# A hybrid decoder layer on one core: when retention starts, how decay tiles are made, and how the first loads are queued

## The chip, the core and the metric

The program runs on one core of a Trainium2 chip. The time is that of one execution in device microseconds (us), median of several; a profiled execution gives the trace. The engines are named as in the profile: PE (matrix products; PEld its weight loads), DVE (vector), ACT (scalar engine, with function tables that must be loaded), POOL and SP (SP issues most DMAs here, in order).

## The reference

One layer, 512 tokens of width 1024, all float32. After an RMS norm one wide projection feeds two token mixers: retention (8 heads) and a gated DeltaNet (8 heads, called DN below). Both are chunked, four chunks of 128 tokens. Their outputs are gated, merged and projected, and a gated MLP with a short causal convolution follows.

```python
u = rmsnorm(h, g_mix); proj = u @ w_in
rq, rk, rv, rgate, dq, dk, dv, dz, db, da, gate_r, gate_d = split(proj)
ro = retention_chunkwise(rotary(rq), rotary(rk) * RET_DK**-0.5, rv)     # 4 chunks, 8 heads
q, k, v = silu(causal_dwconv(concat(dq, dk, dv)))                       # then l2norm of q and k
G = cumsum(g); L[i, j] = exp(G_i - G_j) for i >= j                      # the decay tiles
A = strict_lower((beta * k) @ k.T * L)
u, w = triangular_solve(I + A, [beta * v, beta * k * exp(G)])           # the solve
# a scan over the four chunks then gives the DeltaNet output do
h += (sigmoid(gate_r) * (silu(rgate)*norm(ro) @ w_ret) + sigmoid(gate_d) * (norm(do)*silu(dz) @ w_dn)) @ w_o
h += (silu(a) * b) @ w_down ; a, b = split(causal_dwconv(rmsnorm(h) @ w_up) + bias); out = rmsnorm(h)
```

## The kernel before

Every product is made of three products of split halves: a float32 operand is cut into `hi` (a rounded copy, ACT) and `lo` (what is left, DVE), and PE adds hi·hi, hi·lo and lo·hi in a PSUM bank. Weights come in blocks of 128x1024 (`wraw`), issued by SP in the order of a fixed list and split to `whi` on ACT and `wlo` on DVE. Branch, output and down projections use a Strassen-like scheme with seven products, whose weight sums POOL's DMAs prepare.

The order of the instructions on PE, ACT, DVE and POOL is written down when the program is built. The class `Order` keeps a model clock; small tasks (Python generators) are queued with `spawn`, and after each dense product `poll` lets the tasks record their instructions whose model time has come. A number in a `yield` is a pause in model us, and a `while ...: yield 0.3` waits for a condition. On the chip each engine follows its recorded order and waits only for semaphores. So a changed pause or condition changes which instructions stand next to which, here from the start up to the end of the DN heads. SP's queue has eight semaphores in turn: a DMA is issued when the eighth DMA before it has landed and its own conditions hold.

The places that matter, in time:

- **Head.** `load_x` loads the rows of x transposed (tiles `xt0` to `xt7`, 256 KB each), `load_w` halves of the first two weight blocks, the rest comes in `load_rest`. `g_split` makes `ghi` and `glo` of one tile; in steps named in the dictionary `then` it also writes one column of a tile that is loaded next, by `act.copy`, and since the DMA into this tile must wait for that write, the later loads are held back until ACT is there. `square` feeds the row sums: tiles `sq` are added on DVE, and the matmul `pss` takes the sum. `ba_w` is a small weight that the products `pba` need.
- **DN heads**, two groups of four (GH = 4). Each head takes three weight blocks, products `pk`, `pq`, `pv`, a convolution and Silu (tiles `k`, `q`, `v`), and transposes on PE (`pkt`, `pqt`, `pvt`). `decay_tiles` spawns `decay_tile` for each head: a DMA broadcasts a row into `gb`, ACT makes |G_i - G_j| by four Abs (each with another bias) and then one Exp. Exp and Silu lie in different function tables, so a table is loaded (ACT_TABLE_LOAD) where they follow each other. DVE then builds the tile `A` from `pkk` and `gb`.
- **Solve.** For a group, `solve` runs 31 steps on DVE (the chain: `xtmp`, `xx`), sends the result through DRAM into `tt`, and `solve_up` joins the blocks with products `pm` in four rounds; `m` is their negated copy on DVE. Then two `scan` tasks, for two heads each (`psc`, `vn`, `Sn`), whose ends (`scan_end`) normalise `vtok`, transpose it (`pot`) and copy it with a scale to `doT` on ACT.
- **Retention.** The blocks of rq, rk and rv are products `pr` between the two groups. `ret_back` then does four pairs of heads, `ret_scores` (`prs`, `pkv`), `ret_state` (`rS`), `ret_out` (`pro`) and `ret_norm` (`ro`, `proT`, `roT`).

All PSUM tiles share eight banks; a new tile is given one that is free in the recorded order, and waits on the chip for the last reader of what was in it.

Of the kernel before, what the change touches and what calls it, by code (L numbers as in the profile page):

```python
# [11 lines left out]
F32 = mybir.dt.float32  # L12
F32R = mybir.dt.float32r
AF = mybir.ActivationFunctionType
# [5 lines left out]
P = 128  # L20
T = 512
D = 1024
NT = T // P
# [74 lines left out]
class Order:  # L98
# [29 lines left out]
    def spawn(self, gen, after=0.0):  # L128
        self.n += 1
        heapq.heappush(self.tasks, ((self.clock if self.now is None else self.now) + after, self.n, gen))  # L130
# [107 lines left out]
def body(nc, tc, ctx, io):  # L238
    sp = nc.sync
    order = Order()  # L240
    spawn, poll, hold = order.spawn, order.poll, order.hold
    vec = Engine(order, "vec", nc.vector, vec_cost)
    act = Engine(order, "act", nc.scalar, act_cost)
# [3 lines left out]
    const = ctx.enter_context(tc.tile_pool(name="const", bufs=1))  # L247
# [11 lines left out]
    def S(name, dt=F32):  # L259
        return heap.tile([P, T], dt, name=name, tag="s", bufs=HEAP)  # L260
# [10 lines left out]
    def v3(ap, n=4):  # L271
        return ap.rearrange("p (n f) -> p n f", n=n)
# [5 lines left out]
    def ck(n, f=P):  # L278
        return slice(n * f, (n + 1) * f)
# [8 lines left out]
    def fetch():  # L288

        while count["fetch"] < len(BLOCKS) and free[0]:  # L290
            free[0] -= 1
            i = count["fetch"]
            count["fetch"] += 1
            b = BLOCKS[i]
            n = 512 * b[4] if b[0] == "q" else D
            raw = wp.tile([P, n], F32, name="wraw", tag="wraw", bufs=RAWB)
            if b[0] == "q":
                sp.dma_start(raw, quarter(b[1], b[2])[:, 1024 * b[3]:1024 * b[3] + n])
            else:
                sp.dma_start(raw, io["w"][count["plain"]])  # L300
                count["plain"] += 1
            raws[i] = raw
# [203 lines left out]
    cst = const.tile([P, 256], F32, name="cst")  # L506
# [4 lines left out]
    ones = const.tile([P, P], F32, name="ones")  # L511
# [41 lines left out]
    xt = [S(f"xt{k}") for k in range(KT)]  # L553
# [5 lines left out]
    def load_x(*ks):  # L559
        for k in ks:  # L560
            sp.dma_start(xt[k], io["xt"][k])

    def load_w(i, n):
        sp.dma_start(first_raw[i][:, ck(n, T)], io["w"][i, :, ck(n, T)])

    def load_rest():
        sp.dma_start(cst[:, :P], io["cst"][:, :P])
        sp.dma_start(prm[:, P_CW:], io["prm"][:, P_CW:])
        fetch()
        sp.dma_start(cst[:, P:], io["cst"][:, P:256])  # L570
        sp.dma_start(alog, io["dn_a_log"].partition_broadcast(P))
        sp.dma_start(dtb, io["dn_dt_bias"].partition_broadcast(P))
        sp.dma_start(cst2, io["cst"][:, 256:])

    sp.dma_start(prm[:, :P_BA], io["prm"][:, :P_BA])
    load_x(0)
    load_w(0, 0)
    load_w(1, 0)
    load_x(1)
    sp.dma_start(prm[:, P_BA:P_CW], io["prm"][:, P_BA:P_CW])  # L580


    then = {0: (2, lambda: (load_x(2, 3), load_w(0, 1))), 1: (4, lambda: (load_x(4), load_w(1, 1), load_x(5))),
            2: (6, lambda: (load_x(6, 7), load_rest()))}


    warm = PS("warm")
# [9 lines left out]
    scale, row_scale_, minus = [], [], []  # L597

    def g_split(k):
        act.activation(ghi[k], xt[k], AF.Identity, scale=prm[:, P_GM + k:P_GM + k + 1])  # L600
        if k in then:
            tile_, load = then[k]
            act.copy(xt[tile_][:, :1], ones[:, :1])
            load()
        yield
        vec.scalar_tensor_tensor(glo[k], xt[k], prm[:, P_GM + k:P_GM + k + 1], ghi[k].bitcast(F32), ALU.mult, ALU.subtract)
        yield
        g_ready.add(k)
        spawn(square(k), 0.6)

    def square(k):
        sq = S("sq")
        act.activation(sq, xt[k], AF.Square, scale=1.0 / 32.0)
        yield
        squares.append(sq)
        if len(squares) > 1:
            vec.tensor_tensor(squares[0], squares[0], sq, ALU.add)
            yield
        if len(squares) == KT:
            yield from row_scales(squares[0])  # L620
# [72 lines left out]
    def hn(name):  # L693
        return const.tile([P, H, NT], F32, name=name)
# [4 lines left out]
    beta, G, nG, eG, egl, ekd = (hn(n) for n in ("beta", "G", "nG", "eG", "egl", "ekd"))  # L699
    g_dram = dram.tile([32, P], F32, name="g_dram")  # L700
# [75 lines left out]
    em, egb = {}, {}  # L776

    def row_of(d, h):
        return d[4 * h:4 * h + 4, :].rearrange("n f -> (n f)").partition_broadcast(P)

    def decay_tiles(hs):
        while "G" not in have:
            yield 0.3
        for h in hs:
            while h >= GH and "o" not in heads[h - GH]["got"]:
                yield 0.3
            spawn(decay_tile(h))
            yield 9.0 if h < GH else 4.0

    def decay_tile(h):  # L790
        gb = S(f"gb{h}")
        sp.dma_start(gb, row_of(g_dram, h))
        yield 6.0 if h < GH else 2.6
        for n in range(NT):
            act.activation(gb[:, ck(n)], gb[:, ck(n)], AF.Abs, bias=nG[:, h, n:n + 1])
        act.activation(gb, gb, AF.Exp, scale=-1.0)
        yield
        em[h] = gb

    def conv_silu(ps, ci, name):  # L800
        w = prm[:, P_CW + 4 * ci:P_CW + 4 * ci + 4]
# [11 lines left out]
    GH = 4  # L813
# [18 lines left out]
    heads = [dict(h=h, got=set()) for h in range(H)]  # L832


    keys = [0]
# [84 lines left out]
    def v_front(hd, ps):  # L920
# [8 lines left out]
            act.activation(hd["vtok"][:, ck(n)], pvt[:, ck(n)], AF.Identity, scale=hd["c1"][:, n:n + 1])  # L929
        hd["got"].add("v")  # L930

    def solve(g):

        group = heads[g * GH:(g + 1) * GH]
        while not all("k" in hd["got"] for hd in group):
            yield 0.3
        while g > 0 and not all("o" in hd["got"] for hd in heads[(g - 1) * GH:g * GH]):
            yield 0.3
        sa = [heap.tile([P, 32, 16], F32, name=f"sa{i}", tag="s", bufs=HEAP) for i in range(2)]
        adv = a_dram[g].rearrange("b h n i j -> (b h n) i j")  # L940
        for i in range(2):
            sp.dma_start(sa[i][:NP], adv[:, :, ck(i, 16)])
        xx = small.tile([P, 32, 32], F32, name="xx", tag="xx", bufs=1)
        tmp = small.tile([P, 256], F32, name="xtmp", tag="xtmp", bufs=1)
        pool.memset(xx[:NP], 0.0)
        pool.memset(xx.rearrange("p a b -> p (a b)")[:NP, ::33], 1.0)
        yield 8.0
        for j in range(31):
            shp = [NP, j + 1, 31 - j]
            a = sa[j // 16][:NP, j + 1:, j % 16].unsqueeze(1).to_broadcast(shp)  # L950
            tv, xv_ = v3(tmp[:NP, :(j + 1) * (31 - j)], j + 1), xx[:NP, :j + 1, j + 1:]
            vec.tensor_tensor(tv, a, xx[:NP, :j + 1, j:j + 1].to_broadcast(shp), ALU.mult)
            vec.tensor_tensor(xv_, xv_, tv, ALU.subtract)
            yield
        sp.dma_start(x_dram[g].rearrange("b h n i j -> (b h n) (i j)"), xx[:NP].rearrange("p a b -> p (a b)"))
        for b in range(4):
            sp.dma_start(tt_all[R32[b], :, R32[b]], x_dram[g][b].rearrange("h n j i -> j (h n) i"))
        yield 13.5
        spawn(solve_up(group))
# [191 lines left out]
    normed = []  # L1151
# [3 lines left out]
    def ret_scores(hp):  # L1155

        pss = [PS("prs") for _ in range(2)]
        for n in range(NT):
            for r, ps in zip(E64, pss):
                pe.matmul(ps[:, ck(n)], rkT[n][r, hp], rqT[n][r, hp], start=True, stop=True)  # L1160
        pk = PS("pkv")
        for n in range(NT - 1):
            for e, r in enumerate(E64):
                vv = rv[n][hp // 2][:, ck(2 * hp % 4 + e)]
                pe.matmul(pk[r, ck(n)], krot[n][:, hp, r], vv, start=True, stop=True)
        yield
        states[hp] = [None]
        sTs = [S("sT") for _ in range(2)]
        for sT, ps in zip(sTs, pss):
            vec.tensor_tensor(v3(sT), v3(ps), umask.unsqueeze(1).to_broadcast([P, NT, P]), ALU.mult)  # L1170
        return sTs, pk
# [58 lines left out]
    def ret_back():  # L1230
        while any(a is None for a in (*rqT, *rkT, *(b for a in rv for b in a))):
            yield 0.3
        for hp in range(4):

            while "up" not in heads[GH - 1]["got"] or len(normed) < 2 * hp or keys[0]:
                yield 0.3
            yield 1.5
            sTs, pk = yield from ret_scores(hp)
            yield from ret_state(hp, pk)
            spawn(ret_out(hp, sTs))  # L1240
            yield 8.0
# [23 lines left out]
    def scaled(front, hd, ps):  # L1265
# [5 lines left out]
        yield from front(hd, x)  # L1271

    spawn(decay_tiles(range(GH)))

    def dn_front(g):
# [7 lines left out]
    for front in (rq_front, rk_front, rv_front(0), rv_front(1)):  # L1283
        if front is rk_front:
            spawn(decay_tiles(range(GH, H)), 75.0)
        dense_r([PS("pr") for _ in range(NT)], g_tile, done=front)
    spawn(ret_back())
    dn_front(1)

# [498 lines left out]
```

## Time and profile before

| | us |
|---|---|
| median of 3 runs | 986.39 (984.97 to 987.19) |
| profiled execution | 986.46 |
| its span, first to last instruction | 984.7 |
| PE busy | 965.5 (98% of the span) |
| DVE, ACT, POOL busy | 747.3, 533.9, 166.7 |
| PE in the chain that ended last | 82% of the span |

The span is 1.8 us shorter than the profiled execution's own time. A row of the timeline has the start, the length, the engine, the line, the operation with output and inputs, and in brackets the idle time before it and what ended that. L200 and L235 are lines of helpers through which all instructions go, so groups are told apart by their tiles. The length of a pipelined matmul overlaps with the next one: what one costs in a row is read from start to start.

### The profile page before, as it was taken

The numbers are of one execution on the slowest core, as the hardware profiler recorded it, in microseconds if no ns is written. First come the engines' busy times: TensorE is split into PE (matmuls) and PEld (weight loads), VectorE is DVE, ScalarE is ACT, GpSimd is POOL, SyncE is SP. The second block draws the span as 40 slices with busy tenths as digits, with TensorE's granted clock in tenths as the row PEclk, the third lists the DMA queues.
The fourth block names the chain that finished last, engine by engine and source line by source line (L and its number), as shares of the span: only waits on it lengthen the run. The fifth ranks groups of instructions, "written<-read, shape, count | busy, mean of one in ns | idle before, by whom it ended". The sixth has DMA issues, their size and how long they took to land.

```text
span 984.7 us, 14107 instructions
## 1 busy us (share of the span) xinstructions
PE 965.5 (98%) x5133; PEld 804.9 (82%) x5133; DVE 747.3 (76%) x1359; ACT 533.9 (54%) x1113; POOL 166.7 (17%) x209
## 2 busy tenths in 40 slices
PE   8999999999899999999999999899999999999997
PEld 6887888888788888888888887788888888888886
DVE  6887799458788898675799889865656676678785
ACT  6589422265955433486786546754444333356663
POOL 0121312224443230132000000221122221000001
PEclk9999999999999999999999999999999999999999
DMA  8244569978788695479986754665579999246663
GB/s 269 89 143 125 145 212 206 268 188 214 169 188 229 165 232 152 147 197 263 252 248 191 273 162 158 207 218 193 205 205 216 226 202 202 86 142 193 191 201 118
DMA packets 82949, 189.27 MB, mean 192 GB/s; under 512 B 22912, under 2 KB 31680, under 8 KB 82880
## 3 DMA queue, kind: packets, MB, share of 16 engines
q1 hardware_dynamic: 55360, 123.36, 38.9%
q0 software_dynamic: 27520, 65.02, 30.0%
q8 instruction: 40, 0.66, 0.3%
q14 instruction: 29, 0.24, 0.1%
HBM read 185.17 MB, written 68.19 MB: 257 GB/s over the span
## 4 chain that ended last, share of the span: by engine, by line
PE 82%; DVE 6%; ACT 6%; DMA 3%; issue 3%; POOL 0%; SPq 0%; POOLq 0%; DVEq 0%; ACTq 0%
PE pb L230 12%; PE pa L230 12%; PE py L230 12%; PE pd L230 10%; PE pz L230 9%; PE pr L230 9%; PE psc L230 3%; PE pv L230 3%; PE pk L230 2%; PE pq L230 2%; DVE wlo L200 2%; PE po L230 2%; PE pro L230 1%; ACT whi L200 1%; ACT gb L200 1%
## 5 line engine op out<-in xcount | busy, mean ns | idle before, releaser
L200 ACT CAST whi<-wraw 128x1024 fp32r<-128x1024 f32 (+1 forms) x214 | 220.0, 1030 | 201.7 <-PE pr L230 55.7
L200 DVE TENSOR_TENSOR wlo<-wraw,whi 128x1024 fp32r<-128x1024 f32 (+1 forms) x214 | 254.7, 1192 | 62.7 <-ACT whi L200 62.0
L200 POOL TENSOR_SCALAR tock<-tick 128x1 f32<-128x1 f32 x72 | 34.5, 480 | 407.3 <-ACT tick L200 407.3
L200 DVE SCALAR_TENSOR_TENSOR acc<-pb,prm,acc 128x511 f32<-128x511 f32 (+1 forms) x44 | 33.0, 749 | 57.0 <-ACT acc L200 56.2
L230 PE MATMUL pa<-u2lo,whi 128*128 128x512 f32 (+1 forms) x192 | 71.4, 372 | 0.0
L230 PE MATMUL pa<-u2hi,whi 128*128 128x512 f32 (+1 forms) x192 | 71.4, 372 | 0.0
L230 PE MATMUL pa<-u2hi,wlo 128*128 128x512 f32 (+1 forms) x192 | 71.3, 371 | 0.0
L230 PE MATMUL pb<-u2hi,whi 128*128 128x512 f32 (+1 forms) x184 | 70.0, 380 | 0.0
L230 PE MATMUL pb<-u2lo,whi 128*128 128x512 f32 (+1 forms) x184 | 69.9, 380 | 0.0
L230 PE MATMUL pb<-u2hi,wlo 128*128 128x512 f32 (+1 forms) x184 | 69.9, 380 | 0.0
L230 PE MATMUL py<-whi,oh 128*128 128x512 f32 x160 | 62.9, 393 | 0.0
L230 PE MATMUL py<-wlo,oh 128*128 128x512 f32 x160 | 62.4, 390 | 0.0
L230 PE MATMUL py<-whi,ol 128*128 128x512 f32 x160 | 62.3, 389 | 0.0
L230 PE MATMUL pd<-whi,T 128*128 128x512 f32 (+1 forms) x198 | 55.4, 366 | 0.0
L230 PE MATMUL pz<-ghi,whi 128*128 128x512 f32 x128 | 51.5, 402 | 0.0
L230 PE MATMUL pr<-whi,ghi 128*128 128x512 f32 x128 | 50.9, 398 | 0.0
L230 PE MATMUL pr<-whi,glo 128*128 128x512 f32 x128 | 50.0, 390 | 0.0
L230 PE MATMUL pz<-ghi,wlo 128*128 128x512 f32 x128 | 49.9, 390 | 0.0
L230 PE MATMUL pz<-glo,whi 128*128 128x512 f32 x128 | 49.9, 390 | 0.0
L230 PE MATMUL pr<-wlo,ghi 128*128 128x512 f32 x128 | 49.8, 389 | 0.0
L200 DVE SCALAR_TENSOR_TENSOR acc<-pa,prm,acc 128x511 f32<-128x511 f32 (+1 forms) x44 | 32.9, 749 | 19.0 <-ACT acc L200 18.3
L200 ACT ACTIVATE acc<-pb,prm 128x512 f32<-128x512 f32 x22 | 17.2, 780 | 48.5 <-PE pb L230 48.5
(329 smaller groups left out, 2425.0 us busy)
## 6 DMA issues: line engine op xcount, KB each, us to landing
wraw<-w SPq DMA_DIRECT2D x98, 512.0 KB, 4.5
s<-wm POOLq DMA_DIRECT2D x30, 1024.0 KB, 8.4
wraw<-s SPq DMA_DIRECT2D x60, 512.0 KB, 4.0
s<-wd POOLq DMA_DIRECT2D x24, 704.0 KB, 5.4
wraw<-wm SPq DMA_DIRECT2D x30, 512.0 KB, 4.5
s<-s POOLq DMA_DIRECT2D x10, 1024.0 KB, 11.8
wraw<-wd SPq DMA_DIRECT2D x15, 512.0 KB, 3.6
s<-s POOLq DMA_DIRECT2D x8, 704.0 KB, 9.0
```

Source lines behind the costliest of these rows:

```text
L200: return f(out, *args, **kw)
L230: self.engine.matmul(out, lhsT, rhs, start=start, stop=stop, **kw)
```

## The change

1. A one-element activation on a constant stands first on ACT, so ACT's first table load no longer stands behind the wait for `xt0`.
2. `load_x(2)` moves up into the loads that are issued at once, and the later loads are grouped anew: `xt3`, `xt4` and a half of w0 behind the copy of step 0, `xt5` to `xt7` and a half of w1 behind that of step 1, the rest behind a copy into `cst` at step 3.
3. Decay tiles are made for two heads in one task: two DMAs, eight Abs, two Exp. The pause between tasks is doubled, 18 and 8 instead of 9 and 4.
4. `ret_back` waits for the end of the first solve's chain (`chains`), no longer for `solve_up` (`"up"`).

```diff
+    tick = const.tile([P, 1], F32, name="first")
+    act.activation(tick, ones[:, :1], AF.Square)
...
     sp.dma_start(prm[:, P_BA:P_CW], io["prm"][:, P_BA:P_CW])
+    load_x(2)
-    then = {0: (2, lambda: (load_x(2, 3), load_w(0, 1))), 1: (4, lambda: (load_x(4), load_w(1, 1), load_x(5))),
-            2: (6, lambda: (load_x(6, 7), load_rest()))}
+    then = {0: (3, lambda: (load_x(3), load_w(0, 1), load_x(4))), 1: (5, lambda: (load_w(1, 1), load_x(5, 6, 7))),
+            3: (None, load_rest)}
...
-            act.copy(xt[tile_][:, :1], ones[:, :1])
+            target = cst if tile_ is None else xt[tile_]
+            act.copy(target[:, :1], ones[:, :1])
...
-        for h in hs:
-            while h >= GH and "o" not in heads[h - GH]["got"]:
+        for pair in zip(hs[::2], hs[1::2]):
+            while pair[0] >= GH and not all("o" in heads[h - GH]["got"] for h in pair):
                 yield 0.3
-            spawn(decay_tile(h))
-            yield 9.0 if h < GH else 4.0
+            spawn(decay_pair(pair))
+            yield 18.0 if pair[0] < GH else 8.0
+    def decay_pair(pair):
+        gbs = [S(f"gb{h}") for h in pair]
+        for h, gb in zip(pair, gbs):
+            sp.dma_start(gb, row_of(g_dram, h))
+        yield 6.0 if pair[0] < GH else 2.6
+        for h, gb in zip(pair, gbs):
+            for n in range(NT):
+                act.activation(gb[:, ck(n)], gb[:, ck(n)], AF.Abs, bias=nG[:, h, n:n + 1])
+        for h, gb in zip(pair, gbs):
+            act.activation(gb, gb, AF.Exp, scale=-1.0)
+        yield
+        em.update(zip(pair, gbs))
...
+        chains.add(g)
         sp.dma_start(x_dram[g]...)
...
-            while "up" not in heads[GH - 1]["got"] or len(normed) < 2 * hp or keys[0]:
+            while 0 not in chains or len(normed) < 2 * hp or keys[0]:
```

What it does to the recorded order is shown at three places. The first is the start of SP's queue, in the head. Before:

```order
L575 DMA prm<-prm 128x8
L561 DMA xt_108<-xt 128x512
L564 DMA wraw<-w 128x512 x2
L561 DMA xt_109<-xt 128x512
L580 DMA prm<-prm 128x128
L564 DMA wraw<-w 128x512 x2
L561 DMA xt_110<-xt 128x512
L561 DMA xt_111<-xt 128x512
L561 DMA xt_113<-xt 128x512
L561 DMA xt_112<-xt 128x512
```

The same queue after:

```order
L577 DMA prm<-prm 128x8
L561 DMA xt_108<-xt 128x512
L564 DMA wraw<-w 128x512 x2
L561 DMA xt_109<-xt 128x512
L582 DMA prm<-prm 128x128
L561 DMA xt_110<-xt 128x512
L564 DMA wraw<-w 128x512
L561 DMA xt_111<-xt 128x512
L561 DMA xt_112<-xt 128x512
L564 DMA wraw<-w 128x512
```

The third tile of rows (`xt_110`) now stands ahead of both second halves of the weights, and the half of w1 behind two more tiles.

The second place is ACT in the first group of DN heads. `gb_641` and `gb_739` are the decay tiles of heads 0 and 1 before (`gb_643` and `gb_644` after); `v_657` and `q_613`, or `v_661` and `q_615`, are of head 1, `k_709` or `k_713` of head 2. Before:

```order
L200 ACTIVATE q_613<-q_613 128x512
L200 ACTIVATE k_709<-scaled,prm 128x512
L200 ACTIVATE gb_641<-gb_641,nG 128x128 x4
L200 ACT_TABLE_LOAD
L200 ACTIVATE gb_641<-gb_641 128x512
L200 ACT_TABLE_LOAD
L200 ACTIVATE v_657<-v_657 128x512
L200 ACTIVATE junk,ssqq<-pqt 128x128 x4
L200 CAST whi<-wraw 128x1024
L200 ACTIVATE k_709<-k_709 128x512
L200 ACTIVATE q_780<-scaled,prm 128x512
L200 ACTIVATE gb_739<-gb_739,nG 128x128 x4
```

ACT at the same place after:

```order
L200 ACTIVATE q_615<-q_615 128x512
L200 ACTIVATE k_713<-scaled,prm 128x512
L200 ACTIVATE gb_643<-gb_643,nG 128x128 x4
L200 ACTIVATE gb_644<-gb_644,nG 128x128 x4
L200 ACT_TABLE_LOAD
L200 ACTIVATE gb_643<-gb_643 128x512
L200 ACTIVATE gb_644<-gb_644 128x512
L200 ACT_TABLE_LOAD
L200 ACTIVATE v_661<-v_661 128x512
L200 ACTIVATE junk,ssqq<-pqt 128x128 x4
L200 CAST whi<-wraw 128x1024
L200 ACTIVATE k_713<-k_713 128x512
```

Two tiles are made between one pair of table loads; the second tile moved ahead of `v`, `junk`, `whi` and `k`. Over the whole program there are 16 table loads before and 12 after, all four fewer in this group.

The third place is PE at the end of the first group's scans, where the keys of the second group begin: `pot` transposes the outputs of heads 0 to 3 (`vtok`), `pkt` and `pkk` belong to the keys of heads 4 and 5. Before:

```order
L235 MATMUL pot<-cst,vtok_840 128x128 x4
L235 MATMUL pkt<-cst,k_2527 128x128 x4
L230 MATMUL pkk<-k_2527 128x128 x4
L230 MATMUL pq<-ghi_142,whi 128x512
L230 MATMUL pq<-glo_150,whi 128x512
L230 MATMUL pq<-ghi_142,wlo 128x512
L235 MATMUL pot<-cst,vtok_941 128x128 x4
L230 MATMUL pq<-ghi_143,whi 128x512
L230 MATMUL pq<-glo_151,whi 128x512
L230 MATMUL pq<-ghi_143,wlo 128x512
L235 MATMUL pot<-cst,vtok_1052 128x128 x4
L235 MATMUL pot<-cst,vtok_1230 128x128 x4
```

PE at the same place after, up to the second transpose:

```order
L235 MATMUL pkt<-cst,k_2220 128x128 x4
L230 MATMUL pkk<-k_2220 128x128 x4
L235 MATMUL pot<-cst,vtok_913 128x128 x4
L230 MATMUL pk<-ghi_141,whi 128x512
L230 MATMUL pk<-glo_149,whi 128x512
L230 MATMUL pk<-ghi_141,wlo 128x512
L235 MATMUL pot<-cst,vtok_857 128x128 x4
```

After it come 12 dense products, the third `pot`, 9 more, the fourth `pot`, and 18 products of `pq`: the four transposes moved apart, and only one key (head 4) stands among them. The same place on ACT, before, from the key of head 4 on (`A_2671` and `ktok_2672` read its `pkt`, `A_2694` and `ktok_2695` that of head 5):

```order
L200 ACTIVATE A_2671,ssk<-pkt 128x128 x4
L200 ACTIVATE ktok_2672<-pkt,ekd 128x128 x4
L200 ACTIVATE gb_2607<-gb_2607,nG 128x128 x4
L200 ACT_TABLE_LOAD
L200 ACTIVATE gb_2607<-gb_2607 128x512
L200 ACTIVATE doT_2689<-pot,prm 128x512
L200 ACTIVATE A_2694,ssk<-pkt 128x128 x4
L200 ACTIVATE ktok_2695<-pkt,ekd 128x128 x4
L200 ACTIVATE doT_2729<-pot,prm 128x512
```

And after:

```order
L200 ACTIVATE A_2634,ssk<-pkt 128x128 x4
L200 ACTIVATE ktok_2635<-pkt,ekd 128x128 x4
L200 ACTIVATE rS<-rS,cst_102 128x128
L200 CAST whi<-wraw 128x1024
L200 ACTIVATE gb_2619<-gb_2619,nG 128x128 x4
L200 ACTIVATE gb_2620<-gb_2620,nG 128x128 x4
L200 ACT_TABLE_LOAD
L200 ACTIVATE gb_2619<-gb_2619 128x512
L200 ACTIVATE gb_2620<-gb_2620 128x512
L200 ACTIVATE doT_2667<-pot,prm 128x512
```

The first `doT` moved behind a state update, a weight split and a second decay tile, and the key of head 5 moved away.

More of the change, by code (lines that the diff above doesn't have):

```diff
@@ L783, in decay_tiles @@
             yield 0.3
-        for h in hs:
-            while h >= GH and "o" not in heads[h - GH]["got"]:
+        for pair in zip(hs[::2], hs[1::2]):
+            while pair[0] >= GH and not all("o" in heads[h - GH]["got"] for h in pair):
                 yield 0.3
-            spawn(decay_tile(h))
-            yield 9.0 if h < GH else 4.0
[L790 to L796, printed above, removed]
+            spawn(decay_pair(pair))
[10 more added lines that the diff above has]
+            act.activation(gb, gb, AF.Exp, scale=-1.0)
         yield
-        em[h] = gb
+        em.update(zip(pair, gbs))
     def conv_silu(ps, ci, name):
@@ L930, in v_front @@
         hd["got"].add("v")
+    chains = set()
     def solve(g):
```

## The prediction

> **What bounds the kernel now.** I read the page first (PE is busy 98% of the span and carries 82% of the chain that ended last), then what PE waited for, then the stages in which it waited. The list of PE's waits, longest in total first, has in each row the tile that PE was to write, the engine and tile that it waited for, the total, the count and the longest:
>
> ```profile
> PE pot L235 <- ACT doT L200: 1.5, 1, 1.5
> PE pot L235 <- ACT ktok L200: 1.4, 1, 1.4
> ...
> PE pk L230 <- ACT whi L200: 1.3, 1, 1.3
> ...
> PE pss L230 <- DVE sq L200: 0.7, 1, 0.7
> PE pba L230 <- DVE ba_w L200: 0.7, 1, 0.7
> ...
> PE pqt L235 <- ACT q L200: 0.6, 1, 0.6
> PE pvt L235 <- ACT v L200: 0.5, 1, 0.5
> ...
> PE pkt L235 <- ACT k L200: 0.3, 1, 0.3
> ```
>
> No wait is over 1.5 us. PE does the same work after the change, so the change can win back some of these microseconds, or add others. The two largest lie together, and the stage around them shows ACT as what is late (columns: stretch, length, busy time and count of PE, PEld, DVE, ACT, POOL, then granted clock, DMA share, GB/s):
>
> ```profile
> 242.00:263.00 21.00, 18.14 (x116) 15.42 (x115) 12.44 (x52) 18.79 (x63) 11.43 (x13) 0.92 0.73 155
> ```
>
> The clock of this stage is 0.92, so I cut the stage finer; and the chain through it names the work:
>
> ```profile
> 250.33:253.74 3.41, 0.88 (x5) 0.42 (x4) 3.10 (x13) 3.40 (x15) 0.88 (x2) 1.00 1.06 196
> 253.74:257.15 3.41, 3.08 (x12) 2.69 (x13) 0.00 (x0) 3.38 (x10) 1.52 (x2) 0.50 0.88 192
> ```
>
> ```profile
> 246.10 1.14 ACT A L200 x8
> 247.25 1.03 ACT ktok L200 x4
> 248.28 1.16 ACT gb L200 x4
> ...
> 249.50 1.25 issue
> 250.75 0.63 ACT gb L200
> 251.38 0.58 ACT doT L200
> 251.96 1.03 ACT A L200 x8
> 252.99 1.04 ACT ktok L200 x4
> ...
> 254.07 1.11 PE pot L235 x4
> ```
>
> In one stretch of 3.41 us PE is busy for 0.88, and in the next its clock is granted at half. ACT stands in A, ktok, a decay tile with its table load (the 1.25 of "issue") and the copies that free the banks, and two transposes wait for it. The stall costs 1.5 + 1.4 = 2.9 of waiting, and from 254.07 to 257.15 half speed: 3.08 / 2 = 1.5. Together 4.4 us.
>
> **The third place, the stall.** After the change one key, not two, stands on PE among the four transposes, with dense products between them. I need a price for what PE does there, from start to start:
>
> ```profile
> 442.05 93.89 PE py L230 x414
> ```
>
> ```profile
> 245.90 1.06 PE L230 MATMUL pkk<-k 128*128 128x128 f32 x8
> ...
> 246.80 0.60 PE L235 MATMUL pot<-cst,vtok 128*128 128x128 f32 x4
> ...
> 247.23 0.60 PE L235 MATMUL pkt<-cst,k 128*128 128x128 f32 x4
> ```
>
> A dense product costs 93.89 / 414 = 0.227, pkk 246.80 - 245.90 = 0.90, a transpose of four 0.43. By the recorded waits, the first PE instruction after the change that needs the bank of the first doT is head 4's pqk, behind pkk, four pot, and 3 + 12 + 9 + 18 = 42 products: 0.90 + 1.72 + 9.5 = 12.1 us after pkt. ACT in that time does A 1.14, ktok 1.03, rS (a tile like a quarter of ktok, 0.26), a split, two tiles' Abs 2 x 1.16, a table load 1.28, two Exp 1.26, doT 0.58. The split is the costliest group of ACT:
>
> ```profile
> L200 ACT CAST whi<-wraw 128x1024 fp32r<-128x1024 f32 (+1 forms) x214 | 220.0, 1030 | 201.7 <-PE pr L230 55.7
> ```
>
> With 1.03 the sum is 8.9 us, 3.2 before PE asks. So I take the whole 4.4 as won. Bounds: nothing (the stall turns up a few products later) and 4.4.
>
> [...]
>
> **First group of DN heads.** Four table loads go. The last wait there is for the Silu of head 3's key; these rows are what stands right behind it on ACT before:
>
> ```profile
> 96.03 0.71 ACT L200 ACTIVATE q<-scaled,prm 128x512 f32<-128x512 f32 x1
> 96.64 1.12 ACT L200 ACTIVATE vtok<-pvt,c 128x128 f32<-128x128 f32 x4
> ```
>
> After, these two stand ahead of it and four loads are gone: 4 x 1.28 - 0.71 - 1.12 = 3.3 us earlier, while PE gets to its pkt 9 products earlier (the nine of pr that stood ahead are behind it): 2.0. The 0.3 goes. Head 2's v: two loads fewer (2.6), a second tile more ahead (1.16 + 0.63), and whi, junk and a scaled k behind it (about 2.8, by whi 1.03, ktok 1.03 for junk, q 0.71): 3.6 earlier against PE's 2.0; the 0.5 goes. Head 2's q: two loads fewer, a scaled v (0.71) ahead, 1.9 earlier against 2.0: its 0.6 stays. Won 0.8; bounds 0 and 1.4. What it moves: SP issues the tiles' DMAs in pairs, behind eight writes of A. Silu stays in ACT's order behind a longer block, which the 1.6 left at v must cover.
>
> **The head.** The rows, with idle times:
>
> ```profile
> 4.08 1.28 ACT L200 ACT_TABLE_LOAD   x1 [4.08 <-DMA xt<-xt]
> ...
> 6.75 0.50 PE L230 MATMUL pk<-ghi,whi 128*128 128x512 f32 x1 [1.28 <-ACT whi L200]
> ...
> 7.07 0.62 ACT L200 CAST whi<-wraw 128x512 fp32r<-128x512 f32 x1 [0.38 <-DMA wraw<-w]
> ...
> 9.68 0.41 PE L230 MATMUL pba<-ghi,ba_w 128*32 128x512 f32 x1 [0.71 <-DVE ba_w L200]
> ...
> 22.09 1.05 PE L230 MATMUL pss<-ones,sq 128*128 128x1 f32 x8 [0.74 <-DVE sq L200]
> ```
>
> ```profile
>   DMA xt<-xt: 0.9, 2
> ```
>
> The load leaves the path (it fits before 4.08), and the first product starts about 1.2 earlier. But ACT waits for the second weight until 7.07, and from there whi, ghi, ba_w and pba follow one another in the same order as before; no DMA ahead of that landing has moved. So the first 1.3 is spent waiting at pq and pba, and I count 0 for the table load. The third tile of rows moves two places up the queue, and the two waits of ghi for xt (0.9 together, the tile's list) go; sq's sum comes 0.9 earlier, and the 0.7 at pss goes. Won 0.7; bounds 0 and 2.0 (if w1 lands as much earlier as the load).
>
> **Retention.** PE now does prs and pkv between the second and third round of pm, and the fillers that stood there go elsewhere. No product stands any more between the third and the fourth round:
>
> ```profile
> 198.54 1.15 PE L230 MATMUL pm<-tt,A 64*64 64x64 f32 x32
> ...
> 199.76 0.69 DVE L200 TENSOR_SCALAR m<-pm 128x512 f32<-128x512 f32 x1 [0.29 <-PE pm L230]
> ...
> 201.21 0.97 PE L230 MATMUL pm<-m,ta 64*64 64x64 f32 x26
> ```
>
> Before, PE filled the time of m with six products from 199.62 on. After, it waits from about 199.6 until m is done at 199.76 + 0.69 = 200.45, with the hop 0.9. Cost 0.9; bounds 0 and 2.1 (a split of 1.2 ahead of m). Nothing else of the retention changes in number; what it covers, by the rows, was not idle before.
>
> **The sum.** 986.46 (the profiled execution, 0.1 over the median) - 4.4 - 0.8 - 0.7 + 0.9 = 981.5 us. About 0.2% (2 us) is what a measurement of this kernel can tell from no change.
>
> **Rivals.** *The stall moves.* The pair makes a block of 2 x 1.16 + 1.28 + 1.26 = 4.9 us on ACT where one tile took 3.1, and each Silu, split and doT behind it waits. If the 3.2 us of cover at pqk fail, or the block of heads 6 and 7 meets a product that waits for v or k, PE stalls again and with it the clock: 985.9, no change to be measured. For it: ACT's 18.79 of 21 us. Against: the cover counted above. [...]
>
> *The half clock stays* (another cause than the idle stretch): 983.0. Against it: the half clock begins at once behind the idle stretch.
>
> *w1 lands earlier*, and the table load counts after all: 1.3 less, 980.2.
>
> *The solve comes late* (the other side). These rows are of SP and of the solve's products:
>
> ```profile
> 174.90 0.49 SPq L955 DMA_DIRECT2D x_dram<-xx  x1
> ...
> 180.76 2.64 SPq L957 DMA_DIRECT2D tt<-x_dram  x4
> ```
>
> ```profile
> L230 PE MATMUL pm<-tt,A x192: 190/191/267, 189.0 to 396.5; 32*32 32x32 f32 x128, 64*64 64x64 f32 x64
> ...
> DMA to landing us min/median/max: 1.9/3.2/5.1
> ```
>
> The last tt was issued by 183.4 and landed 3.2 later by the median, 186.6, and pm came at 189.0: 2.4 to spare. After, pm stands 24 + 3 products earlier, 6.1 us. If the chain on DVE does not get earlier, PE waits 3.7 and loses up to 1.7 by the clock: 986.9. Slower than before by 2 us it is from the point where the chain ends 1.5 later than before; 3 us later gives 989.9, since each further microsecond is PE's. For it: 31 steps must thread through the same DVE. Against: head 3's key, which the chain needs last, comes 3 us earlier on ACT and 9 products earlier on PE.
>
> **How the numbers follow.** My sum 0.57, with its own range 979.7 to 983.6 (first group, head and pm at their bounds); the stall moves 0.20; the half clock stays 0.07; w1 earlier 0.08; the solve late 0.08. The first, third and fourth are faster by more than 0.2%, less a little that spills over: 0.70. No change 0.21, slower 0.09. The range reaches from 979.0 to 986.4.
>
> **What would show it.** Stall: no PE wait for doT or ktok, and a clock of 1.00 from 240 to 260. First group: 12 table loads, PE waits for q alone. Head: the first pk at 5.5, pba still near 9.7, no wait at pss. Retention: one wait of pm for m near 0.9. Wrong would be any new wait over 1.5 us between 60 and 330, a second row with half clock, or a pm that waits for tt.

## The result: 979.9 us, and where the 6.2 us came from

| | before | after |
|---|---|---|
| median of 4 runs each, us | 986.11 (984.97 to 987.19) | 979.92 (979.19 to 981.06) |
| profiled execution, us | 986.46 | 980.2 |
| its span, us | 984.7 | 978.3 |
| PE busy, us | 965.5 | 963.4 |

The ratio is 0.9938, 95% interval 0.9924 to 0.9951: faster by 6.2 us, where 4.9 were forecast. In a second study the changed kernel took 980.53 (six runs, ratio 0.9938, 0.9923 to 0.9952), where 979 to 980 was expected.

The rows of the list of PE's waits, after, that answer to those shown of before (tile that PE was to write, engine and tile waited for, total, count, longest):

```profile
PE pba L230 <- DVE ba_w L200: 1.7, 1, 1.7
...
PE pm L230 <- DVE m L200: 0.8, 1, 0.8
...
PE pqt L235 <- ACT q L200: 0.4, 1, 0.4
PE psc L230 <- ACT tt L200: 0.3, 1, 0.3
```

No pot waits for doT or ktok, no pkt for k, no pvt for v, no pss for sq. Three waits are new or longer: pm for `m`, psc for `tt`, and pba for `ba_w` (the last is 0.7, as before, in the profile of the second study). The stage that was 18.14 us busy at a clock of 0.92 is now, by the windows of after:

```profile
242.00:263.00 21.00, 21.00 (x124) 17.89 (x123) 15.87 (x27) 20.28 (x46) 6.94 (x9) 1.00 0.66 151
```

ACT, the fourth of the busy times, is busier than before (20.28 against 18.79), and PE loses nothing by it. The chain that ended last runs here through PE alone:

```profile
239.01 0.44 PE pkt L235 x4
239.44 0.89 PE pkk L230 x8
240.34 0.44 PE pot L235 x4
240.78 0.70 PE pk L230 x3
241.47 0.44 PE pot L235 x4
241.91 2.77 PE pk L230 x12
...
247.64 4.10 PE pq L230 x18
```

To place the gain I read the start of the same product in both timelines. Before (its pss stands in the prediction, at 22.09), then after:

```profile
143.53 0.60 PE L235 MATMUL prkT<-cst,krot 128*128 128x128 f32 x4
...
585.00 0.62 PE L230 MATMUL po<-whi,mB 128*128 128x512 f32 x2
...
978.42 0.28 PE L230 MATMUL pd<-wlo,T 128*128 128x256 f32 x1
```

```profile
21.36 1.05 PE L230 MATMUL pss<-ones,sq 128*128 128x1 f32 x8
...
141.01 0.60 PE L235 MATMUL prkT<-cst,krot 128*128 128x128 f32 x4
...
578.50 0.62 PE L230 MATMUL po<-whi,mB 128*128 128x512 f32 x2
...
971.99 0.28 PE L230 MATMUL pd<-wlo,T 128*128 128x256 f32 x1
```

At these four places PE has done the same number of products in both, tile by tile. The differences are -0.73, -2.52, -6.50 and -6.43. So in these two executions the head gave 0.7, the stretch with the first group of DN heads 1.8, the stretch with solve, retention and second group 4.0, and the rest nothing.

### The profile page after: what moved, and what is told of

It is laid out like the page before. It is cut to its first block, busy times and chain, and to the rows that moved or that the text cites. A ratio compares the mean times of both kernels' runs of the same rounds, so it can differ in the third digit from the quotient of the medians.

```text
span 978.3 us, 14091 instructions
## 1 busy us (share of the span) xinstructions
PE 963.4 (98%) x5133; PEld 804.6 (82%) x5133; DVE 748.2 (76%) x1359; ACT 529.1 (54%) x1110; POOL 165.1 (17%) x209
## 4 chain that ended last, share of the span: by engine, by line
PE 85%; DVE 6%; ACT 4%; DMA 2%; issue 2%; POOL 0%; SPq 0%; POOLq 0%; DVEq 0%; ACTq 0%
PE pb L230 12%; PE pa L230 12%; PE py L230 12%; PE pd L230 10%; PE pz L230 9%; PE pr L230 9%; PE pq L230 3%; PE pv L230 3%; PE psc L230 3%; PE pk L230 3%; DVE wlo L200 2%; PE po L230 2%; PE pro L230 1%; ACT whi L200 1%; PE pm L230 1%
```

## Experiments

Edits are against the kernel before, unless the text says otherwise. All were timed in five rounds beside it; "clock" is the mean granted clock, listed for each run. The last three columns are read as above, from each kernel's own profiled execution against that of before: start of pss, pss to prkT, prkT to po.

| kernel | median us | ratio, 95% interval | clock in the runs | pss | pss to prkT | prkT to po |
|---|---|---|---|---|---|---|
| before | 986.4 to 986.7 | 1 | 0.995 to 0.999 | 0 | 0 | 0 |
| the change, twice | 979.92, 980.53 | 0.9938 (0.9923 to 0.9952) | 0.999 to 1.000 | -0.7, -1.0 | -1.8, -1.6 | -4.0, -4.1 |
| e1: head | 985.49 | 0.9993 (0.9980 to 1.0006) | 0.995 to 0.999 | -0.9 | -0.5 | +0.6 |
| e2: pairs | 979.04 | 0.9923 (0.9908 to 0.9939) | 0.997 to 0.998 | -0.5 | -2.1 | -5.2 |
| e3: retention | 981.69 | 0.9953 (0.9937 to 0.9968) | 0.997 to 1.000 | -0.2 | -0.4 | -4.2 |
| e4: head, pairs | 979.10 | 0.9924 (0.9907 to 0.9941) | 0.997 to 0.999 | +0.8 | -1.9 | -4.8 |
| g3: pairs, retention | 981.56 | 0.9949 (0.9937 to 0.9960) | 0.996 to 0.999 | +0.6 | -2.0 | -4.0 |
| f2: zeros in the stall | 986.21 | 0.9997 (0.9985 to 1.0009) | 0.995 to 0.999 | 0.0 | -0.2 | -0.4 |
| f3: pairs, heads 0 to 3 | 980.64 | 0.9952 (0.9934 to 0.9970) | 0.996 to 1.000 | +0.1 | -1.7 | -4.2 |
| f4: pairs, heads 4 to 7 | 989.93 | 1.0040 (1.0025 to 1.0055) | 0.993 to 0.997 | -0.1 | +1.5 | +1.9 |
| g1: pairs, loads | 979.22 | 0.9926 (0.9914 to 0.9938) | 0.998 to 0.999 | -0.8 | -1.8 | -4.6 |
| g2: head, pairs, warm | 977.91 | 0.9914 (0.9902 to 0.9926) | 0.998 to 0.999 | -1.7 | -2.0 | -4.7 |
| g4: zeros in both | 985.08 | 0.9986 (0.9978 to 0.9995) | 0.998 to 1.000 | +0.4 | -0.5 | -1.9 |

The table shows a scatter too: where code is unchanged (e2, e3, f2, f3, f4, g3), pss starts from 0.5 earlier to 0.6 later. The last three columns come from one execution each.

### The parts alone

e1 is edits 1 and 2, e2 edit 3, e3 edit 4, e4 edits 1 to 3, as in the diff above.

> Before, with the head's part alone (table load first, three tiles of rows at once). Theory (each part pays where it stands): the first pk about 0.9 earlier, pba where it was, pss 0.7 earlier, and everything behind it shifted by 0.7 with nothing else changed: -0.7 us, 985.4, the stall at 250 with its half clock still there. Rival (the whole gain is one reshuffle of the order, each part alone changes little): the order behind the head is the same as before, so the 0.7 is lost again in later waits: 0.0.

The head gains 1.45 up to prkT, and then it loses: the profiled execution spends two stretches of 3.41 us at half clock behind the stall, not one. Its windows (busy time and count of PE, PEld, DVE, ACT, POOL, then clock, DMA share, GB/s):

```profile
248.10:251.52 3.42, 1.67 (x10) 0.95 (x8) 3.35 (x14) 3.41 (x12) 1.56 (x2) 1.00 1.09 195
251.52:254.93 3.41, 2.31 (x8) 1.91 (x9) 0.54 (x3) 3.38 (x12) 1.62 (x2) 0.50 0.85 162
254.93:258.34 3.41, 3.41 (x14) 2.92 (x13) 0.69 (x1) 3.10 (x6) 0.00 (x0) 0.50 0.66 174
```

The interval holds both -0.7 and 0, so the head alone isn't settled by the time.

> Before, with the decay pairs alone. Theory: in the first group PE's lost time goes from about 2.2 to 0.6 us (prkT 1.8 earlier than before, counted from pss). In the recorded order pairs alone already leave one key, not two, in front of the pot of heads 0 to 3, so the stall at 250 goes too, or shrinks to one wait of about 1 us for doT, since twelve pot stand in a row without a dense product: -1.8 -2.5 to -4.4, so 980 to 982, clock 1.00. Rival (the stall goes by the retention's earlier start, and a block of 4.9 us on ACT makes it worse): -1.8 only, 984.3, with a half clock still in the records near 250.

Pairs alone are worth all of the change: 979.04, 1 us below the range of the theory. No pot waits for doT or ktok.

> Before, with the retention's earlier start alone. Theory: first group and head as before, the stall at 250 gone (one key stands in front of the four pot), and between the third and the fourth round of pm stand fourteen pro, so no wait of 0.8 for m: -3.5 to -4.4, 982 to 982.6, clock 1.00. Rival (the stall moves): table loads of single decay tiles still stand on ACT between doT and ktok, PE waits elsewhere between 230 and 300 for 1.5 or more: -1 or less, above 985.

As the theory had it, though 981.69 lies 0.3 below its range: the stall is gone, and pm does not wait for m. So each of two edits takes the stall away without the other; together they can't do it twice.

> After, without the retention's earlier start. Theory (the parts add): e1 plus e2, within 0.3 us. If the stall goes by pairs alone, this is 979.3 to 981.3, equal to the whole change; if the retention is what takes the stall away, it is 983.6 with the stall. Rival (parts do not add): a shift of 0.7 in the head changes which transfer meets which wait, and the sum is off by over 1 us.

979.10 lies 0.2 below the theory's range, and by the ratios the sum of e1 and e2 would be 978.2: 0.9 apart and not 0.3, though the intervals allow it. The head adds nothing that can be measured to pairs. Half of e4's runs stand at 0.998 or below (979.8 to 981.5), the others at 0.999 (977.3 to 978.4). Its profile, one of the slower runs, shows a half clock in the head:

```profile
6.29:9.70 3.41, 1.91 (x6) 0.68 (x5) 1.56 (x3) 2.29 (x6) 0.00 (x0) 1.00 0.90 320
9.70:13.12 3.42, 3.19 (x8) 2.33 (x9) 3.02 (x6) 3.32 (x7) 0.00 (x0) 0.50 1.03 328
```

PE starts earlier (the first pk at 5.82, where before has 6.75), then waits in the head 1.1 for whi and 0.7 for `ba_w`, and half clock follows.

### What makes the stall: the order or the table loads

```diff
-        for h in hs:
+        for pair in (zip(hs[::2], hs[1::2]) if hs[0] < GH else zip(hs)):   # f3; f4 has >= for <
...
+            spawn(decay_pair(pair) if len(pair) == 2 else decay_tile(pair[0]))
+            yield (9.0 if pair[0] < GH else 4.0) * len(pair)
```

> Before, with decay pairs for heads 0 to 3 alone and single tiles for heads 4 to 7. Theory (the pairs of the first group move 21 products of pr and pk past the first pm and shift the whole order behind it, so that one key, not two, stands ahead of the four pot): nearly the whole gain of pairs alone, -6 to -7.5, 979 to 980.5, no half clock near 250. Rival (the stall goes since two table loads and their tiles no longer stand on ACT among ktok and doT, which only pairs of heads 4 to 7 bring): -1.9 only, 984.5, with waits for doT or ktok over 1 us left.

> Before, with decay pairs for heads 4 to 7 alone. In the recorded order the two keys still stand ahead of the pot as before, and the pair of heads 4 and 5 makes a block of 4.9 us on ACT. Theory (the order, not the number of table loads, makes the stall): the stall stays with waits for doT or ktok of 1 us and more and with half clock, 985.5 to 988. Rival (the table loads make it): stall gone, -4 to -5, 981.5 to 982.5.

f3 touches no decay tile of heads 4 to 7, and the stall is gone (-4.2 from prkT to po; 980.64, 0.1 above the theory's range). In f4 the two keys still stand ahead of the pot, and the stall grows (989.93, 2 us above the theory's range). Its waits and its chain:

```profile
PE pot L235 <- ACT ktok L200: 4.8, 1, 4.8
```

```profile
249.80 0.58 ACT doT L200
250.38 2.31 ACT gb L200 x8
...
252.75 1.26 issue
254.00 1.15 ACT gb L200 x2
255.15 1.03 ACT A L200 x8
256.18 1.04 ACT ktok L200 x4
...
257.27 1.12 PE pot L235 x4
```

The block of the pair on ACT, 2.31 + 1.26 + 1.15 = 4.7, is the one for which I had worked out 4.9.

f4 does not have fewer table loads, as its rival supposes: it has 16 like before, and between 230 and 280 there are two in each of the kernels (from 249.5 and 266.2 before, 246.0 and 256.7 after, 238.6 and 256.1 in f3, 252.7 and 270.0 in f4). So their number can't be what makes the stall; where they stand can. In f3 the first tile stands on ACT ahead of head 4's key, and `doT` follows `ktok` at once:

```profile
239.87 0.63 ACT L200 ACTIVATE gb<-gb 128x512 f32<-128x512 f32 x1
...
242.23 1.16 ACT L200 ACTIVATE ktok<-pkt,ekd 128x128 f32<-128x128 f32 x4
243.23 1.90 ACT L200 ACTIVATE doT<-pot,prm 128x512 f32<-128x512 f32 x3
```

It is the same in e2 and e3. In after and g3 the block stands between ktok and doT as in f4, but only one key stands there, and PE has products and transposes meanwhile (in after from 241.91 to 251.58, 9.7 us of work). So the recorded order makes the stall: it goes when one key is left and the block stands ahead of it, and also when the block stays behind the one key and PE has other work. Two keys without the block between them were not tried.

### The half clock

f2 puts a product with a weight of zeros, into the bank of the dense product that is open, seven times ahead of the third pot and four times ahead of the fourth; g4 also four times ahead of pss.

```diff
+        pots.append(h)
+        for _ in range({3: 7, 4: 4}.get(len(pots), 0)):
+            nc.tensor.matmul(open_bank[0], zr, ghi[0], start=False, stop=False)
         pt = transpose4(o, "pot")
...
+        for _ in range(4):                                    # g4 only
+            nc.tensor.matmul(open_bank[0], zr, ghi[0], start=False, stop=False)
         pss = PS("pss")
```

> Before, with eleven more products in the stall: seven ahead of the third pot of heads 0 to 3 and four ahead of the fourth, with a weight of zeros into the bank of the pq that is open there, so that they add nothing; the rest of the order is unchanged. Theory (the half clock follows a window in which PE is mostly idle): both waits turn into work of the same length, no row with half clock is left before the end, granted clock 0.998 to 0.999 in nearly all runs, and the time is 1 to 1.5 below before: 985 to 985.5. Rival (the half clock has another cause, such as the load on DMA or ACT): half clock near 254 as before, 986.4 to 986.7.

> Before, with the eleven products of zeros in the stall as in f2, and four more ahead of pss (into the open bank of pk), where PE waits for sq. Theory (before's runs scatter from 983.7 to 989.5 since each of two idle places, 22 and 250, is followed by a half clock in some runs and not in others): granted clock 0.998 or more in nearly all runs, 984 to 985, scatter under 2 us. Rival (the half clock comes without idle stretches too): clock 0.995 to 0.997 in half the runs, 986 to 987.

In f2's profile the stall's two windows are full and at full clock, at the same load on ACT and DMA as before:

```profile
250.33:253.74 3.41, 3.23 (x16) 2.19 (x14) 3.04 (x13) 3.40 (x15) 0.89 (x2) 1.00 1.09 201
253.74:257.15 3.41, 3.12 (x20) 2.73 (x21) 0.60 (x1) 3.38 (x9) 1.46 (x2) 1.00 0.87 180
```

But over the runs f2 missed: the median moved by 0.5 with an interval that holds no change. The clock listed for each run tells more. It is a mean over the whole span, and at the end, where PE is done, the clock is half for 0.9 to 3.9 us in the kept traces. The ten traces without a half clock ahead of that end have 0.998 to 1.000, the four with one 0.993 to 0.997. By this mark five of f2's twelve runs still have a half clock (0.997 or less), against fifteen of the seventeen of before beside them. No trace of those five was kept, but there is a second idle place, the wait at pss, and f4's profile shows what it can do (first two rows; the other three are its stall):

```profile
19.22:22.64 3.42, 2.11 (x13) 1.34 (x11) 2.91 (x5) 1.63 (x3) 0.00 (x0) 1.00 0.98 388
22.64:26.05 3.41, 3.41 (x11) 2.67 (x12) 2.25 (x4) 1.04 (x1) 2.30 (x5) 0.50 0.83 280
251.33:254.74 3.41, 1.17 (x8) 0.76 (x6) 2.03 (x7) 3.38 (x8) 1.23 (x2) 1.00 0.99 164
254.74:258.15 3.41, 0.88 (x5) 0.88 (x5) 0.00 (x0) 3.41 (x15) 0.00 (x0) 0.50 0.71 129
258.15:261.57 3.42, 3.42 (x12) 2.65 (x11) 0.00 (x0) 1.76 (x4) 0.00 (x0) 0.50 0.02 5
```

One such stretch cost 1.5 us there: f4's prkT is 1.5 later than before's, from the same code. With both places filled (g4) all twelve runs stand at 0.998 or more, where fifteen of the seventeen of before beside them stand at 0.997 or less, and the time falls by 0.14% (985.08, 0.1 above the theory's range) though PE does fifteen products more. So in these runs the half clock goes with the idleness at the two places; the rival with DMA or ACT falls, as their load in f2's two windows is that of before (ACT busy for 3.40 and 3.38 in both kernels, DMA share 1.09 and 0.87 against 1.06 and 0.88).

### The head and a better version

```diff
+                for _ in range(2 if k == 0 else 0):           # g2, in first_blocks behind mm3
+                    nc.tensor.matmul(warm[:, :P], ones, ones, start=True, stop=True)
```

g1 is edits 2 and 3, g2 edits 1 to 3 with these four products, g3 edits 3 and 4.

> Before, with decay pairs and the new order of the first loads, but without the early table load and without the retention's earlier start. Theory (the early table load only lets PE start pk 0.9 earlier and then stand idle for 1.7 ahead of pba; the loads take the gap at pss): first pk near 6.7, no wait at pss over 0.3, no half clock in the head, granted clock 0.998 or more in nearly all runs, and 977.5 to 978.5. Rival (the early table load is worth something): 979 or more, later than pairs with both.

> Head and pairs as in e4, and four more warm-up products in the first waits of the head: two behind the first three pk and two behind the first three pq, into the warm-up's bank. Theory (what spreads e4's runs from 977.3 to 981.5 is a half clock that follows the idle stretch ahead of pba, between 6 and 10 us): granted clock 0.998 or more in all runs, and 977.5 to 978.5, the level of the undisturbed runs of e4. Rival (the spread has another cause): median 979 and the same spread; if the four products stand in the way, 980.

> Pairs and retention together, without the head's part: the change less its head. Theory (the retention adds a wait of 0.8 for m and takes away nothing that pairs alone leave): slower than pairs alone (979.0), 980 to 980.7, and with half clock in the head's gap at pss in some runs. Rival (the retention's earlier start adds a gain of its own to pairs): below 979, so that the head would have cost something in the whole change.

g1: pss comes 0.8 earlier without the early table load, so that load alone is worth nothing that the runs show; 979.22 is 0.7 above the theory's range and no better than e4. g2 is the best of all, 977.91, with all runs between 977.5 and 978.72 where e4's lay between 977.3 and 981.5. Its start, by the timeline:

```profile
7.25 0.64 PE L1264 MATMUL warm<-ones 128*128 128x128 f32 x4
...
8.41 0.61 PE L1264 MATMUL warm<-ones 128*128 128x128 f32 x4
8.78 0.47 PE L230 MATMUL pba<-ghi,ba_w 128*32 128x512 f32 x1
```

The first pba lies between 8.95 and 9.93 in the others, and pss, here at 20.37, at 21.08 or later. In this execution that is mostly an early load: ACT starts the second split of weights, right behind the landing, at 5.93, against 6.97 to 7.36 in e1, e4 and the change's second execution, and `ba_w` follows it on ACT. What the four products may be credited with is the narrower spread and the clock of 0.998 or more in all five runs.

g3 is slower than pairs alone by 2.5 us of median (the intervals meet at 0.9937 to 0.9939), and 0.9 above the theory's range. From prkT to po every kernel with pairs and retention gains 4.0 to 4.1, those with pairs for all heads and no retention 4.6 to 5.2. Of the waits that e2, e4 and g1 don't have, g3 has the 0.8 of pm for m, as the change has, and this one:

```profile
PE pot L235 <- DVE vtok L200: 1.2, 1, 1.2
```

The wait for vtok, near 435, is not new: before has it with 1.1, and e3 too. Pairs without the retention's earlier start lose it, and wait 0.3 to 1.4 for `res` ahead of po instead. So the retention's earlier start took the stall away when it was alone, and by these columns it costs 0.6 to 1.2 us on top of pairs, in part since a gain of pairs that has nothing to do with the stall is lost again.

The head comes off differently by the company it has: 1.0 to 1.6 us of median on top of g3 (the change against g3), nothing on top of e2, 0.7 alone. None of the three is clear of its intervals.

## Why the prediction was right, and where it was off

**The stall** (forecast -4.4). Right, and by the recorded order: one key ahead of the pot, products between them. The cover at pqk held (these rows are of after's timeline): pqk stands 12.7 us behind the pkt at 238.84, where I had worked out 12.1, and the first doT is done at 249.05, 2.5 us ahead of it, where I had 3.2.

```profile
248.38 0.67 ACT L200 ACTIVATE doT<-pot,prm 128x512 f32<-128x512 f32 x1
...
251.58 1.05 PE L230 MATMUL pqk<-q,k 128*128 128x128 f32 x8
```

The size: retention alone, which leaves pm without a wait, gives 4.2 from prkT to po and has a wait of 1.0 for `res` ahead of po that before has at 0.4; with it the stall is worth 4.2 to 4.8. Part of that wait is scatter, as f2, with the order of before, has it at 1.2. Before's own rows, from start to start (250.16, 252.01 and 254.07, less 0.23 and 0.43), give 1.6 for each of the two waits and with the 1.5 of half speed 4.7. The prediction doesn't say which edit moves the key. Edit 3 does it alone, even for heads 0 to 3 alone (f3), and so does edit 4.

"No wait is over 1.5 us" was a misreading: the first row of before's list, which the prediction doesn't show, is pt for hs, 2.0 in two waits, the longest 1.6. It lies between 600 and 640, is the same after, and bears on no term.

**Retention's wait** (forecast +0.9). There, at the place and nearly at the size:

```profile
192.49 1.15 PE L230 MATMUL pm<-tt,A 64*64 64x64 f32 x32
194.44 1.22 PE L230 MATMUL pm<-m,ta 64*64 64x64 f32 x32 [0.80 <-DVE m L200]
```

Stall and pm together were forecast at -3.5, and the stretch measured -4.0. Two smaller waits that I had not counted trade places in it: psc waits 0.3 for tt after, and the 0.4 that pmt waited for res before is gone. pm did not wait for tt, so "the solve comes late" did not occur.

**First group** (forecast -0.8, bounds 0 and 1.4). This is the term that was mis-sized: -1.8 between pss and prkT. About 0.4 of it is before's own execution, which lost more there than others of the same code (-0.4 in e3, -0.2 in f2, -0.5 in g4); kernels with pairs lie at -1.6 to -2.1, so pairs are worth about 1.4, my upper bound. The step of the sum that failed is to take a recorded wait for what it costs. Before, at head 2's q:

```profile
79.86 0.40 PE L230 MATMUL pq<-ghi,wlo 128*128 128x512 f32 x1
80.87 0.66 PE L235 MATMUL pqt<-cst,q 128*128 128x128 f32 x4 [0.61 <-ACT q L200]
```

The recorded idle time is 0.61, but from start to start it is 1.01, and a product takes 0.227: the loss is 0.78. By the same reading v's 0.5 and k's 0.3 are 0.62 and 0.47, and a loss of 0.31 ahead of a pkt stands under no wait of the list that I quoted: 2.2 in all. q's wait, which I left at 0.6, is 0.4 after, and 0.6 in the second execution.

**The head** (forecast -0.7). Right as to place (the wait at pss is gone) and near in size (-0.7, and -1.0 in the second execution). The early table load is spent ahead of pba, as I had counted, but in after not by the wait for the second weight that I had named: this landed 0.9 earlier (the split starts at 6.21, not 7.07), and then ACT waited for the second tile of rows:

```profile
0.79 1.28 ACT L200 ACT_TABLE_LOAD   x1 [0.79 <-PEq L1789]
...
7.87 0.72 ACT L200 ACTIVATE ghi<-xt,prm 128x512 fp32r<-128x512 f32 x1 [1.04 <-DMA xt<-xt]
...
9.77 0.42 PE L230 MATMUL pba<-ghi,ba_w 128*32 128x512 f32 x1 [1.65 <-DVE ba_w L200]
```

A difference of 0.7 between two executions is hardly more than pss moves in unchanged code; but of the six kernels with edit 2 (the change's two executions among them) five have pss 0.7 to 1.7 earlier, and the sixth is e4 with its half clock. So the gain at pss is likely, and its size open. What I had not counted is the clock: with no wait at pss and no stall, the ten runs of the change stand at 0.999 or 1.000, where before's stand mostly at 0.995 to 0.998, and g3's, which lack the head, at 0.996 to 0.999.

**The half clock.** I took the idleness in the stall as what brings it, by the row with 0.88 busy, and the runs bear that out: in f2's profile the stall's two windows are at 1.00, and the change stands at 0.999 to 1.000 in its ten runs. f4's two stretches of half clock begin at 22.64 and 254.74, 232.10 us apart, which is 68 times 3.413, the length of before's stretch by its trace (253.74 to 257.15). The start in before, 253.74, lies 1.0 us off f4's steps, and e4's, 9.70, lies 0.7 off; two starts in one execution are too few to tell a step from chance. The same stall is followed by half clock for 3.41 us in before and for 6.83 in e1 and f4.

**The sum.** 979.9 against 981.5: the first group was worth 1.0 more than I had counted and the stretch with stall and pm 0.5 more. The bounds as I wrote them add up to 978.7 and 984.2, not 979.7 and 983.6; the result lies inside both. That it came near 980.2, the price of the rival "w1 lands earlier", is chance: pba starts no earlier in the profile of the change (9.77 against 9.68).

## What to carry to other kernels

Size a wait by the time from the start of the product ahead of it to the start of the waiting one, less what that product takes in a row; the idle time in brackets left out about 0.16 us of each of the first group's four here. Look in the recorded order for what stands on one engine between two releases that PE needs in a row, and test each part of a change alone: two of these edits cured the same stall, and one of them costs something on top of the other. Behind windows in which PE idled for 1.3 us (f4's at pss) and 2.5 us (before's stall), half clock cost another 1.5 us each (prkT later by that in f4, 3.08 / 2 in before), and by the clocks it came in some executions and not in others (in fifteen of before's seventeen beside f2, in five of f2's twelve): compare the granted clock run by run before a difference of 2 us is explained.

## What the runs showed of the hardware

Half clock followed windows of 3.41 us in which PE was busy for 0.88 (before), 1.17 and 2.11 (f4), 1.67 (e1) and 1.91 us (e4), and, at half clock, 0.88 (f4) and 2.31 (e1). The busy time alone does not say when it comes: after windows with 1.86 (before) and 1.85 (e2), which follow, the clock stayed at 1.00.

```profile
632.62:636.03 3.41, 1.86 (x17) 1.66 (x16) 1.71 (x4) 1.10 (x4) 2.06 (x3) 1.00 0.81 240
636.03:639.44 3.41, 3.41 (x31) 3.27 (x30) 2.54 (x9) 2.66 (x10) 1.19 (x2) 1.00 0.89 333
```

```profile
625.04:628.45 3.41, 1.85 (x16) 1.65 (x16) 1.55 (x3) 1.27 (x4) 2.06 (x3) 1.00 0.82 240
628.45:631.87 3.42, 3.42 (x30) 3.28 (x29) 2.55 (x9) 2.67 (x10) 1.03 (x2) 1.00 0.97 376
```

These are windows of matrix products with transposes at another time of the kernel; what tells them from the others is left open.
